# An attention layer's event table: memory loads behind the key copy, output transposes 12 to 15 steps later, last memory mixing and samples' norm moved

## The chip, the core and the metric

The kernel runs on one core of a Trainium2 chip. The metric is the device time of one execution in microseconds (us). Before the change it is 1348.73 us, the median of three runs (1347.39 to 1349.89).

TensorE is called PE here as in the profile; DVE is VectorE, ACT ScalarE, POOL GpSimd, and SP the SyncE queue, which issues the DMAs. Every engine works through its own instructions in program order, and semaphores order the engines against each other.

## The reference

A two-layer encoder trunk for one step: layer 0 mixes tokens with a recurrence (RWKV-7), layer 1 with differential attention. Each layer does one input projection, mixes, attends to a memory of 256 rows with four "memory heads", gates, and does one output projection. 512 prompt rows and 32 sample rows are computed together. The change touches layer 1 alone:

```python
def diff_layer(x, mk, mv, k_past, v_past, layer_idx, ...):
    h = rmsnorm(x, norm_w)
    q, k, v, qm, gate = jnp.split(h @ w_in, [...], axis=-1)
    ...
    # per head: softmax(q1 k1) - lam * softmax(q2 k2), masked, times v
    o = rmsnorm(o, subln) * (1.0 - lam_init)
    y_mem = mem_attention(qm, mk, mv)        # 4 heads, 256 memory rows
    out = jnp.concatenate([o, y_mem], axis=-1) * jax.nn.silu(gate)
    return x + out @ w_out, k, v
```

The prompt rows attend to prompt keys and use memory keys made in this kernel; the 32 sample rows also use cached keys and values (128 rows) and cached memory keys and values (256 rows).

## The kernel before, in words

**Main stream.** Layer 1 is written as one stream of PE matmuls, the input projection: each block of 128 output columns is 48 matmuls (weights 128x128, 272 rows of tokens at a time; `6 * KT = 48`). One such matmul is called a step. Twelve attention heads follow each other; head h owns three blocks (value, key, query), some gate blocks, and in heads 1, 3, 5 and 7 (`MEM1`) the query and gate of a memory head. The function `begin(h)` gives the step at which a head starts: heads 7, 8, 9, 10 and 11 start at steps 1632, 1872, 2064, 2208 and 2352, for example. After step 2688 the output projection follows.

**Events.** Everything else (transposes, scores, softmax, copies, DMAs, norms) is an event: `at(pos, fn)` in `diff_layer` (from L2041) puts a function into the list `ev`, the list is sorted, and each function is called just before step `pos` of the stream. Its instructions then stand at that place in the program of every engine that it uses. There is no other scheduler: tables of numbers at the file's head set the order. "h9+122" below means 122 steps after the start of head 9.

**One head's events on the SP queue.** The prompt's weights stream in all the time as `h16s` tiles. Head h then sends, at fixed steps: at +99 the keys are made, at +108 `keys_out` (L2122) copies the half of the keys across partitions (`kh<-kh`, two DMAs, needed by the scores `ps_s` from +160 on) and stores the keys (`scr<-sg`, four). At +112 `weights_out` (L2191) of the head before stores its attention weights (`ptr<-pk`, four DMAs of 160 KB), and at +168 `weights_back` reads them back transposed (`aT<-ptr`).

**Memory heads.** `mem_steps` (L1233) is a generator whose pieces are called at the offsets of `MEMAT1` (L41; the last memory head has `MEMAT1B`, L42). The second piece issues four loads on SP: `cmt` (cached memory keys), `mhk`, `mhv`, `cmv`. The third, at +180, transposes `cmt` on PE into the PSUM tile `ps_ck`. Scores, softmax and turning follow, and the last piece is the mixing: `ps_mo` on PE, then two DVE operations that write the gated tile `og`.

**Groups of four heads.** Attention outputs are normalized and transposed for four heads at a time, while the heads after them run: `norms` (L2308), then for j = 0 to 3 `scaled` (L2313, DVE `ot`) and `finished` (L2327: four PE transposes into `ps_oT`, then two DVE operations that write the gated tile `og`). For the second group (heads 4 to 7) that falls into heads 9 and 10, for the last one to the end of head 11. `gated_square` (L1428, ACT, at `GSQUARE`) and `gated_scales` (L1434, at `GSCALE`) take a scale from the finished tiles; the latter's PE result is `ps_gs`.

**Samples.** Also once in four heads the samples' attention is computed (`SAMPLE1`, L53, and `SAMPLE2`, L54, for the last group): scores, mixing, `sample_norm` (L2296, ten small DVE operations on `os`) and `sample_rows` (L2302, PE transpose `ps_osT`). In head 9, `cached_keys` (L2244) transposes the cached keys of the next group on DVE (`to<-ck`) at h9+4; the load of `ck` is issued at h8+152.

**PSUM.** `ps_ck`, `ps_mo`, `ps_oT`, `ps_osT` and `ps_gs` come from one pool, `psm`, of two banks: a tile waits until the one but last of them is read out.

All instructions are recorded through a small wrapper, so that rows of the profile show line 138 (139 after the change) whatever function issued them; the names of tiles tell them apart.

Of the kernel before, what the change touches and what calls it, by code (L numbers as in the profile page):

```python
# [37 lines left out]
GATES1[11] = (8, 9, 10, 11)  # L38
MEM1 = (1, 3, 5, 7)
TILES1 = ((160,180),(188,210),(220,244),(254,280))  # L40
MEMAT1 = (60, 64, 180, 276, 294, 306, 324, 330, 346, 362, 402, 414, 426, 476, 552)  # L41
MEMAT1B = MEMAT1[:8] + (352, 366, 400, 412, 428, 470, 590)  # L42
LOADS1, SPLITS1 = (1, 14), (2, 5, 8, 11)
STAT1, SPREAD1, POWER1, SCALE1 = (14, 27), 12, 32, (37, 41)
SPLITS2, SCALE2 = (7, 11, 13, 17), (33, 36)
GSQUARE = ((8, 36), (8, 132), (9, 36), (9, 84), (10, 10), (10, 32), (10, 56), (10, 78))
GSCALE = ((9, 132), (10, 92))
KVOUT = 164
GSPLIT = ((10, 36, 57), (10, 66, 89), (11, 33, 57), (11, 66, 89), (11, 222, 230), (11, 254, 262), (11, 290, 298), (11, 318, 325))
ORDERED = (2 * KT - 2) * 6 * KT + 3 * KT  # L50
EXP = float(1 << 23)
ROOT = float(0x5F3759DF) + 14 * EXP
SAMPLE1 = ((310, "s"), (338, "m"), (362, "t"), (386, "w"), (406, "n"), (464, "r"))  # L53
SAMPLE2 = ((186, "s"), (214, "m"), (228, "t"), (264, "w"), (311, "n"), (336, "r"))  # L54
TILES2 = ((152, 180), (210, 236), (240, 268), (272, 304))
BACK1, SUMS1, NORM1 = 80, 160, 52
# [84 lines left out]
class Trunk:  # L141
# [1899 lines left out]
    def diff_layer(self, dq, p, mp, mctx, pool_early, tiles, consume):  # L2041
# [8 lines left out]
        def at(pos, fn):  # L2050
            ev.append((pos, len(ev), fn))
# [13 lines left out]
        def make_v(st):  # L2065
            def make(w):
                st["v"] = dq.tile([P, T], F32, tag="v", name="v", bufs=KB)
                yield from self.steps(w, copied(st["v"], w[2]))
            return make

        def make_k(st):
            def make(w):
                st["k"] = dq.tile([P, T], F32, tag="k", name="k", bufs=KB)
                yield from self.steps(w, copied(st["k"], w[2]))
            return make

        def make_q(st):
            def make(w):
                st["qp"] = qp = dq.tile([P, 2, T], F32R, tag="qp", name="qp", bufs=QB)

                def parts(ps, c):
                    for m in range(2):
                        self.ae.activation(qp[rows[m], m, c], ps[rows[m], :], AF.Copy, scale=w[2][rows[m]])
                    if c.start:
                        self.ae.activation(st["G"]["qs"][:, st["j"], :], ps[:, TH - TS :], AF.Copy, scale=w[2])
                    for m in range(2):
                        self.ve.scalar_tensor_tensor(qp[rows[1 - m], m, c], ps[rows[m], :], w[2][rows[m]],
                                                       qp[rows[m], m, c].bitcast(F32), ALU.mult, ALU.subtract)
                yield from self.steps(w, parts)
            return make  # L2090

        def make_gate(g):
            def make(w):
                half[g] = w[2]
                self.ve.tensor_scalar(subg[:, g : g + 1], self.subs, w[2], None, ALU.mult)
                yield from self.steps(w, self.gate_evac(self.o1[g], w[2])[2])
            return make
# [125 lines left out]
        def opened(G, hg):  # L2223
            G["scr"] = [self.dp.tile([T, 4, P], F32, tag=f"scr{i}", name=f"scr{i}", bufs=3) for i in range(2)]
            G["on"] = []
# [94 lines left out]
        def turned_stored(G, j):  # L2320
            G["ot", j] = G["ot", j]()
# [5 lines left out]
        def finished(G, hg, j):  # L2327
            if hg < OTURN:
                x = G.pop(("oT", j))[:].rearrange("p t q -> p (t q)")
            else:  # L2330
                ps = self.psm.tile([P, 512], F32, tag="m", name="ps_oT")
                for t in range(4):
                    self.te.transpose(ps[:, t * P : t * P + P], G["on"][j][:, t, :], self.ident[:])
                x = ps[:]
            g = self.o1[4 * hg + j]
            n = 4 * hg + j
            self.ve.scalar_tensor_tensor(g[:, :TP], x, subg[:, n : n + 1], g[:, :TP], ALU.mult, ALU.mult)
            self.ve.scalar_tensor_tensor(g[:, TP:], G["oT"][:, 32 * j : 32 * j + 32], half[n], g[:, TP:], ALU.mult, ALU.mult)
# [10 lines left out]
        for h, st in enumerate(sts):  # L2349
            f, hg, G = len(makes) * 6 * KT, h // 4, groups[h // 4]  # L2350
            start.append(f)
            makes += [make_v(st), make_k(st), make_q(st)] + [make_gate(g) for g in GATES1.get(h, ())]
            if h % 4 == 0:
                at(f, lambda G=G, hg=hg: opened(G, hg))
                at(f + 97, lambda G=G: sample_open(G))
                at(f + 152, lambda G=G, hg=hg: cached(G, hg))
            if h % 4 == 1:
                for off, fn in ((4, cached_keys), (14, cached_stored), (78, cached_back)) if CTURN else ((124, cached_turned),):
                    at(f + off, lambda G=G, fn=fn: fn(G))
            for off, fn in ((52, values_turn), (62, lambda st: st["vout"]()), (99, keys), (108, keys_out)):  # L2360
                at(f + off, lambda st=st, fn=fn: fn(st))
            last = h == DH - 1
            for t, (x, y) in enumerate(TILES2 if last else TILES1):
                at(f + x, lambda st=st, t=t: scores(st, t))
                at(f + x + 6, lambda st=st, t=t: powers(st, t))
                at(f + (y - (14, 0, 0, 10)[t] if last else y), lambda st=st, t=t, fn=joined if last else turned: fn(st, t))
                if last:
                    at(f + y + 12, lambda st=st, t=t: turned_here(st, t))
            back, sums = (BACK2, SUMS2) if h >= DH - 2 else (BACK1, SUMS1)
            for off, fn in ((124, values_back),) if last else ((y + min(18, back - 2), values_back), (y + (8 if h == DH - 2 else OUT7[0] if h == 7 else OUT1), weights_out), (y + (OUT7[1] if h == 7 else back), weights_back)):  # L2370
                at(f + off, lambda st=st, fn=fn: fn(st))
            if h == 7:
                sums = OUT7[2]
            at(f + y + (SUMS3 if last else sums), lambda st=st: weighted(st))
            at(f + y + (SUMS3 + 11 if last else sums + 14), lambda st=st: squared(st))
            if h in MEM1:
                m = MEM1.index(h)
                makes += [make_query(mems[m]), make_mem_gate(mems[m], m)]
                for off in MEMAT1B if h == MEM1[-1] else MEMAT1:
                    at(f + off, lambda m=m: next(mits[m], None))  # L2380
            if h % 4 == 3:
                for off, fn in (SAMPLE2 if last else SAMPLE1):
                    fn = {"s": sample_scores, "m": sample_mixed, "t": sample_turned, "w": sample_weighted, "n": sample_norm, "r": sample_rows}[fn]
                    at(f + off, lambda G=G, fn=fn: fn(G))
                b = f + y + NORM2 if last else begin(h + 2) + (NORM1 if h < 4 else NORM1B)
                at(b, lambda G=G: norms(G))
                for j in range(4):
                    if hg >= OTURN and not last:
                        x = b + 18 + (14, 24)[hg] * j
                        at(x, lambda G=G, j=j: scaled(G, j))  # L2390
                        at(x + (36 + 10 * j, 38)[hg], lambda G=G, hg=hg, j=j: finished(G, hg, j))
                    elif last:
                        at(b + 18 + 8 * j, lambda G=G, j=j: scaled(G, j))
                        at(b + 48 + 14 * j, lambda G=G, hg=hg, j=j: finished(G, hg, j))
                    else:
                        x = b + 18 + STEP * j
                        at(x, lambda G=G, j=j: (scaled(G, j), turned_out(G, j)))
                        at(x + 10, lambda G=G, j=j: turned_stored(G, j))
                        at(x + GAP1, lambda G=G, j=j: turned_back(G, j))
                        at(x + GAP2, lambda G=G, hg=hg, j=j: finished(G, hg, j))  # L2400
            if h == 10:
                we = []
                at(f + 34, lambda: (mctx.close(), we.append(pool_early())))
        for g, (h, off) in enumerate(GSQUARE):
            at(begin(h) + off, lambda g=g: self.gated_square(g))
        for g, (h, x, y) in enumerate(GSPLIT):
            at(begin(h) + x, lambda g=g: self.gated_split(g, we[0], tiles))
            at(begin(h) + y, lambda g=g: self.gated_rest(g, tiles))
        for g, (h, off) in zip((0, 4), GSCALE):
            at(begin(h) + off, lambda g=g: self.gated_scales(g, 4))  # L2410
# [129 lines left out]
```

## Time and profile before

| what | value |
|---|---|
| profiled execution, its own time | 1346.43 us |
| its span (first to last instruction) | 1343.9 us |
| lies around the span | 2.5 us |
| runs | 1347.39, 1348.73, 1349.89 us |
| mean granted TensorE clock | 0.992 |
| PE busy | 96% of the span |
| DVE, ACT, POOL busy | 71%, 66%, 50% |
| mean DMA rate | 128 GB/s |
| HBM read, written | 130.84 MB, 41.92 MB |

How to read it: a timeline row gives the start in us, the duration in us, the engine, the operation, what it writes and reads, and how many like it stand in the row; brackets at the end give the idle time ahead of it and what ended that. An SP row (SPq) is the issue of a DMA, not its transfer. A row of the waits names who waited for whom, the total in us, the number of waits, and the longest. A row of the windows gives, after the stretch and its length, the busy time of PE, PEld, DVE, ACT and POOL (with instructions), then the granted clock, the DMA engines' busy share and GB/s. Layer 1's stream runs from about 824 us to 1233 us, its last group and the output projection from there to 1344 us.

### The profile page before, as it was taken

Reading aid. Unit: us, or ns where it says so; the run is one execution under the profiler, and the core shown is the slowest. Engines: PE = TensorE matmul, PEld = TensorE weight load, DVE = VectorE, ACT = ScalarE, POOL = GpSimd, SP = SyncE. Lnnn points to the kernel's source line nnn. Section 1 sums busy time; section 2 is a strip of 40 time slices with the busy share of each in tenths; the row PEclk is TensorE's granted clock in tenths of the full one; section 3 lists DMA queues with packets and bytes.
Section 4 is the critical chain, followed back from the end, with each engine's and each line's share of the span. In section 5 each row is a group of like instructions: output and inputs, shape, how many; then the busy total and the mean of one; then the engine's idle time right before and its main releaser. Section 6 shows DMA issues by size and latency. Waiting matters only on the chain. (4 is left out here: it accounts for less than half of the span.)

```text
span 1343.9 us, 32356 instructions
## 1 busy us (share of the span) xinstructions
PE 1295.0 (96%) x11776; PEld 1169.3 (87%) x11776; DVE 950.2 (71%) x2483; ACT 888.6 (66%) x2412; POOL 676.6 (50%) x1139
## 2 busy tenths in 40 slices
PE   6999999999999999999999999999999999999996
PEld 6998989999999999888899999888887887788885
DVE  6767667887788777767575355656698667987855
ACT  6665677777777867656564337777666777886752
POOL 1317765577557655860021007756555655654651
PEclk9999899999999999999999999999999999999998
DMA  7643223322322332233347445777777768874741
GB/s 236 187 115 82 63 71 88 79 67 80 88 68 65 81 101 62 60 81 98 124 150 224 132 130 153 173 175 165 155 177 170 169 164 179 174 166 115 225 149 67
DMA packets 418298, 171.55 MB, mean 128 GB/s; under 512 B 195209, under 2 KB 402578, under 8 KB 418138
## 3 DMA queue, kind: packets, MB, share of 16 engines
q1 hardware_dynamic: 417994, 168.96, 48.7%
q8 instruction: 92, 1.51, 0.5%
q14 instruction: 68, 0.56, 0.1%
q10 hardware_dynamic: 144, 0.52, 0.1%
HBM read 130.84 MB, written 41.92 MB: 129 GB/s over the span
## 5 line engine op out<-in xcount | busy, mean ns | idle before, releaser
L138 PEld LDWEIGHTS <-whs 128*128 128x128 f16 x3456 | 327.0, 98 | 67.2 <-issue 5.2
L138 PE MATMUL ps_g<-h,whs 128*128 128x272 f16 x2688 | 332.0, 279 | 1.3 <-POOL whs L138 1.3
L138 PE MATMUL ps_g<-hh,wlo 128*128 128x272 f32 x912 | 277.4, 304 | 1.3 <-DVE wlo L138 1.3
L138 PE MATMUL ps_g<-hh,whi 128*128 128x272 f32 x912 | 274.6, 301 | 0.9 <-ACT hh L138 0.9
L138 PE MATMUL ps_g<-hl,whi 128*128 128x272 f32 x912 | 270.9, 297 | 0.6 <-POOL hl L599 0.5
L888 POOL TENSOR_TENSOR tm<-u,m 102x84 f32<-102x84 f32 (+23 forms) x372 | 156.5, 421 | 164.4 <-DMA m<-sc 136.4
L138 PEld LDWEIGHTS ps_g<-hh,whi 128*128 128x128 f32 x912 | 174.2, 191 | 4.4 <-ACT hh L138 1.3
L138 PEld LDWEIGHTS ps_g<-hh,wlo 128*128 128x128 f32 x912 | 173.6, 190 | 4.8 <-DVE wlo L138 2.1
L138 PEld LDWEIGHTS ps_g<-hl,whi 128*128 128x128 f32 x912 | 173.5, 190 | 2.4 <-POOL hl L599 0.7
L890 POOL TENSOR_TENSOR u<-u,tm 102x84 f32<-102x84 f32 (+23 forms) x372 | 159.7, 429 | 29.1
L138 POOL TENSOR_TENSOR whs<-h16s,whs 128x512 f16<-128x512 f32 x126 | 147.8, 1191 | 51.1 <-ACT whs L138 45.9
L138 DVE TENSOR_TENSOR wlo<-raw,whi 128x512 fp32r<-128x512 f32 x178 | 128.8, 734 | 47.3 <-ACT whi L138 46.3
L138 ACT CAST whi<-raw 128x512 fp32r<-128x512 f32 x178 | 107.0, 616 | 35.3 <-issue 19.4
L138 POOL TENSOR_SCALAR h16s<-h16s 128x512 f32<-128x512 f32 x112 | 81.4, 739 | 91.9 <-DVE h16s L138 91.9
L138 ACT CAST whs<-h16s 128x512 f16<-128x512 f32 x144 | 84.7, 618 | 31.7 <-POOL h16s L138 30.1
L138 PE MATMUL ps_g<-hl,whs 128*128 128x272 f16 x768 | 93.2, 279 | 0.5 <-POOL whs L138 0.5
L138 ACT ACTIVATE junkw<-h16s 128x512 bf16<-128x512 f32 x138 | 86.4, 627 | 5.7 <-DMA h16s<-in_df_in_dram 5.3
L138 DVE SCALAR_TENSOR_TENSOR SB<-ps_c,dl,sd 64x64 f32<-64x64 f32 x168 | 47.4, 282 | 42.2 <-PE ps_c L138 38.2
L138 PE MATMUL ps_g<-lo,whi 128*128 128x272 f32 x256 | 73.9, 289 | 0.7 <-DVE lo L138 0.7
L138 PE MATMUL ps_g<-hi,whi 128*128 128x272 f32 x256 | 73.7, 288 | 0.0
L138 PE MATMUL ps_g<-hi,wlo 128*128 128x272 f32 x256 | 73.5, 287 | 0.0
L138 ACT COPY sv<-ps_c 64x64 f32<-64x64 f32 x192 | 39.3, 205 | 39.1 <-PE ps_c L138 37.3
(413 smaller groups left out, 2934.5 us busy)
## 6 DMA issues: line engine op xcount, KB each, us to landing
raw<-in_rw_in_dram SPq DMA_DIRECT2D x114, 256.0 KB
h16s<-in_df_in_dram SPq DMA_DIRECT2D x112, 256.0 KB
raw<-in_w_out_dram SPq DMA_DIRECT2D x32, 256.0 KB
h16s<-in_w_out_dram SPq DMA_DIRECT2D x32, 256.0 KB
ptr<-pk SPq DMA_DIRECT2D x44, 160.0 KB
aT<-ptr SPq DMA_DIRECT2D x11, 640.0 KB
scr<-sg SPq DMA_DIRECT2D x96, 68.0 KB
out_dram<-scr SPq DMA_DIRECT2D x6, 1024.0 KB
```

The source lines that it names most:

```text
L138: return lambda *a, **k: self.trunk.tie(self, issue(*a, **k))
L888: nc.gpsimd.tensor_tensor(tm[:, :n, :wd], u3[:, :n, kx : kx + 1].to_broadcast(sh), m3[:, kx : kx + 1, kx + 1 :].to_broadcast(sh), ALU.mult)
L890: nc.gpsimd.tensor_tensor(u3[:, :n, kx + 1 :], u3[:, :n, kx + 1 :], tm[:, :n, :wd], ALU.add)
```

## The change

Five edits, all to offsets of events; no operation is added or removed.

1. `MEMAT1[1]`, also used by `MEMAT1B`, goes from 64 to 124: the four memory loads of heads 1, 3, 5 and 7 are issued 60 steps later. The transposes that read `cmt` stay at +180.
2. The last entry of `MEMAT1B` goes from 590 to 554: the last memory head's mixing moves from h10+14 to h9+122.
3. The new table `SAMPLE1B` holds for the second group: `sample_norm` goes from h8+166 to h9+8, `sample_rows` from h9+32 to h9+44.
4. The second group's `finished` goes from h9+132, h10+12, h10+36, h10+60 to h9+146, h10+26, h10+50, h10+74, with its `GSQUARE` and `GSCALE` entries.
5. The last group's `finished` goes 12 steps later (four times).

```diff
-MEMAT1 = (60, 64, 180, 276, 294, 306, 324, 330, 346, 362, 402, 414, 426, 476, 552)
-MEMAT1B = MEMAT1[:8] + (352, 366, 400, 412, 428, 470, 590)
+MEMAT1 = (60, 124, 180, 276, 294, 306, 324, 330, 346, 362, 402, 414, 426, 476, 552)
+MEMAT1B = MEMAT1[:8] + (352, 366, 400, 412, 428, 470, 554)
...
-GSQUARE = ((8, 36), (8, 132), (9, 36), (9, 84), (10, 10), (10, 32), (10, 56), (10, 78))
-GSCALE = ((9, 132), (10, 92))
+GSQUARE = ((8, 36), (8, 132), (9, 36), (9, 84), (10, 24), (10, 46), (10, 70), (10, 93))
+GSCALE = ((9, 132), (10, 106))
...
 SAMPLE1 = ((310, "s"), (338, "m"), (362, "t"), (386, "w"), (406, "n"), (464, "r"))
+SAMPLE1B = SAMPLE1[:4] + ((440, "n"), (476, "r"))
...
-                for off, fn in (SAMPLE2 if last else SAMPLE1):
+                for off, fn in (SAMPLE2 if last else SAMPLE1 if h < 4 else SAMPLE1B):
...
-                        at(x + (36 + 10 * j, 38)[hg], lambda G=G, hg=hg, j=j: finished(G, hg, j))
+                        at(x + (36 + 10 * j, 52)[hg], lambda G=G, hg=hg, j=j: finished(G, hg, j))
...
-                        at(b + 48 + 14 * j, lambda G=G, hg=hg, j=j: finished(G, hg, j))
+                        at(b + 60 + 14 * j, lambda G=G, hg=hg, j=j: finished(G, hg, j))
```

On SP, in head 3 (heads 1, 5 and 7 are alike): `cmt`, `mhk`, `mhv`, `cmv` are the memory loads, `vt` the values read back, `scr` the keys' store. Before:

```order
L138 DMA cmt<-in_cache_mem_k_dram 128x2x128
L138 DMA mhk<-mkv_11874 128x256
L138 DMA mhv<-mkv_12091 128x256
L138 DMA cmv<-in_cache_mem_v_dram 128x2x128
L138 DMA h16s<-in_df_in_dram 128x4x128
L138 DMA vt<-scr_12367 128x4x128
L138 DMA kh<-kh 64x544 x2
L138 DMA scr_12366<-sg_83 32x17x32 x4
L138 DMA h16s<-in_df_in_dram 128x4x128
L138 DMA ptr<-pk 32x40x32 x4
L138 DMA h16s<-in_df_in_dram 128x4x128 x2
```

On SP, in the same place of head 3, now:

```order
L139 DMA h16s<-in_df_in_dram 128x4x128 x2
L139 DMA vt<-scr_12367 128x4x128
L139 DMA kh<-kh 64x544 x2
L139 DMA scr_12366<-sg_83 32x17x32 x4
L139 DMA h16s<-in_df_in_dram 128x4x128
L139 DMA ptr<-pk 32x40x32 x4
L139 DMA cmt<-in_cache_mem_k_dram 128x2x128
L139 DMA mhk<-mkv_11874 128x256
L139 DMA mhv<-mkv_12091 128x256
L139 DMA cmv<-in_cache_mem_v_dram 128x2x128
L139 DMA h16s<-in_df_in_dram 128x4x128 x2
```

The four loads moved from ahead of the key copy `kh<-kh` to a place behind it, behind the four stores `scr` and behind the four large stores `ptr<-pk`.

On DVE, at the end of head 8, the samples' norm before (`os` and `nt` are its tiles, `og` a gate, `ps_s` the scores of head 8):

```order
L138 TENSOR_REDUCE snm<-ps_s 128x1 x2
L138 TENSOR_SCALAR os_16620<-os_16620 128x1 x2
L138 SCALAR_TENSOR_TENSOR nt_16862<-os_16620 128x1
L138 TENSOR_TENSOR nt_16862<-nt_16862,os_16620 128x1
L138 SCALAR_TENSOR_TENSOR os_16620<-nt_16862,os_16620 128x1
L138 TENSOR_TENSOR nt_16862<-os_16620 128x1
L138 TENSOR_TENSOR nt_16862<-nt_16862,os_16620 128x1
L138 SCALAR_TENSOR_TENSOR nt_16862<-nt_16862 128x1
L138 SCALAR_TENSOR_TENSOR os_16620<-nt_16862,os_16620 128x1
L138 TENSOR_SCALAR os<-os,os_16620 128x128
L138 SCALAR_TENSOR_TENSOR og_12336<-og_12336,ps_g 128x272
L138 STREAM_TRANSPOSE to<-mp 128x256
```

On DVE, at the start of head 9, the samples' norm now (`to<-ck` is the transpose of the cached keys):

```order
L139 TENSOR_REDUCE snm<-ps_s 128x1 x2
L139 SCALAR_TENSOR_TENSOR og_12336<-og_12336,ps_g 128x272
L139 STREAM_TRANSPOSE to<-ck 128x512
L139 TENSOR_SCALAR os_16620<-os_16620 128x1 x2
L139 SCALAR_TENSOR_TENSOR nt_16946<-os_16620 128x1
L139 TENSOR_TENSOR nt_16946<-nt_16946,os_16620 128x1
L139 SCALAR_TENSOR_TENSOR os_16620<-nt_16946,os_16620 128x1
L139 TENSOR_TENSOR nt_16946<-os_16620 128x1
L139 TENSOR_TENSOR nt_16946<-nt_16946,os_16620 128x1
L139 SCALAR_TENSOR_TENSOR nt_16946<-nt_16946 128x1
L139 SCALAR_TENSOR_TENSOR os_16620<-nt_16946,os_16620 128x1
L139 TENSOR_SCALAR os<-os,os_16620 128x128
```

The norm moved across the border of heads 8 and 9 and now stands right behind `to<-ck`.

## The prediction

> **What bounds the kernel now.** I read the page first, then the stretch of layer 1's main stream in the windows, with one window inside head 1, and then whom PE waits for from 824 us to the end.
>
> ```profile
> PE 1295.0 (96%) x11776; PEld 1169.3 (87%) x11776; DVE 950.2 (71%) x2483; ACT 888.6 (66%) x2412; POOL 676.6 (50%) x1139
> ```
> ```profile
> 824.00:1233.00 409.00, 403.03 (x3512) 337.06 (x3512) 290.16 (x874) 297.35 (x819) 243.24 (x248) 1.00 0.74 168
> 863.00:872.00 9.00, 8.98 (x78) 7.45 (x77) 4.55 (x19) 8.19 (x23) 7.95 (x9) 1.00 0.99 215
> ```
> ```profile
> PE ps_oT L138 <- DVE ot L138: 2.0, 2, 1.1
> PE ps_g L138 <- POOL whs L138: 1.8, 3, 0.8
> PE ps_s L138 <- DMA kh<-kh: 1.0, 1, 1.0
> ...
> PE ps_mo L138 <- DVE og L138: 0.9, 1, 0.9
> PE ps_s L138 <- ACT pt L138: 0.9, 1, 0.9
> ```
>
> PE is the bound: busy for 403.03 of the stream's 409.00 us. So what happens on another engine counts only where PE is made to wait. The edits aim at five of these waits, some 5 us in all, and that is all they can win. The second window shows what they may disturb: behind the keys of head 1 the DMA engines are 0.99 busy. A load that joins the queue there waits for what is ahead of it.
>
> **Edit 1: the memory loads.** They now stand on SP behind `ptr<-pk`. `aT<-ptr` reads what `ptr` wrote, so SP's issue of `aT` marks when `ptr` has landed. Here are SP and PE in head 1, then in head 3, and SP's wait ahead of `kh<-kh` in head 3:
>
> ```profile
> 868.48 3.69 SPq L138 DMA_DIRECT2D ptr<-pk  x4
> ...
> 875.21 0.37 SPq L138 DMA_DIRECT2D aT<-ptr  x1
> ```
> ```profile
> 871.34 0.38 PE L138 MATMUL ps_ck<-ident,cmt 128*128 128x128 f32 x2
> ```
> ```profile
> 938.18 3.64 SPq L138 DMA_DIRECT2D ptr<-pk  x4
> ...
> 944.86 0.37 SPq L138 DMA_DIRECT2D aT<-ptr  x1
> ```
> ```profile
> 940.98 0.97 PE L138 MATMUL ps_g<-h,whs 128*128 128x272 f16 x7
> 941.79 0.38 PE L138 MATMUL ps_ck<-ident,cmt 128*128 128x128 f32 x2
> ```
> ```profile
> SPq L138 <- ACT kh L138: 2.2, 1, 2.2
> ```
>
> In head 3 the issue of `ptr` ends at 938.18 + 3.64 = 941.82, so `cmt`, now next, is issued just when PE wants it (941.79). Does a load queued behind `ptr` land ahead of it? Head 8 has such a case, a weight load right behind `ptr`, with ACT waiting for it:
>
> ```profile
> 1122.38 0.98 SPq L138 DMA_DIRECT2D h16s<-in_df_in_dram  x1
> ...
> 1127.39 0.44 SPq L138 DMA_DIRECT2D aT<-ptr  x1
> ```
> ```profile
> 1127.63 0.63 ACT L138 ACTIVATE junkw<-h16s 128x512 bf16<-128x512 f32 x1 [1.30 <-DMA h16s<-in_df_in_dram]
> ```
>
> It was issued at 1122.38 and used at 1127.63, that is 5.25 us later and 0.24 after `aT`'s issue. So it came in the queue's order, and I put `cmt` at `aT`'s issue + 0.3. PE works in order, so the whole stream stops at `ps_ck`. Heads 5 and 7, the span of the four issues in head 5 among them:
>
> ```profile
> 1004.20 0.52 SPq L138 DMA_DIRECT2D cmt<-in_cache_mem_k_dram  x1
> ...
> 1006.24 0.46 SPq L138 DMA_DIRECT2D ckT<-spread  x1
> ...
> 1021.53 0.37 SPq L138 DMA_DIRECT2D aT<-ptr  x1
> ```
> ```profile
> 1017.84 0.38 PE L138 MATMUL ps_ck<-ident,cmt 128*128 128x128 f32 x2
> ```
> ```profile
> 1090.57 0.37 SPq L138 DMA_DIRECT2D aT<-ptr  x1
> ```
> ```profile
> 1087.97 0.38 PE L138 MATMUL ps_ck<-ident,cmt 128*128 128x128 f32 x2
> ```
>
> The four issues take 1006.24 - 1004.20 = 2.0 us of SP, by which what follows them can be early now. In heads 3 and 7 it can't: SP waits 2.2 us for ACT's `kh` there (the row above; head 7 has the same), and an earlier SP only waits longer. In heads 1 and 5 I take the 2.0 off; taking nothing off is the upper end. Head 5's `ps_ck` comes 1.0 earlier, since its wait for `kh<-kh` (1.0) goes.
>
> - Head 1: 875.21 - 2.0 + 0.3 - 871.34 = 2.2 (up to 4.2).
> - Head 3: 944.86 + 0.3 - 941.79 = 3.4.
> - Head 5: 1021.53 - 2.0 + 0.3 - (1017.84 - 1.0) = 3.0 (up to 5.0).
> - Head 7: 1090.57 + 0.3 - 1087.97 = 2.9.
>
> Sum +11.5 (to 15.5), and -1.0 for `kh<-kh`. The lower end is in the rivals. The other three loads and the `aT` behind them are used at +276 and +248, at least 68 steps behind `ps_ck`; at 0.116 us a step (seven from 940.98 to 941.79) that is 7.9 us, so they stay hidden, and would cost about the 2.0 of their issue if that cover were gone.
>
> **Edits 2 to 4: heads 9 and 10.** The samples' norm, and what it meets:
>
> ```profile
> 1132.63 0.27 PE L138 MATMUL ps_osT<-ident,os 128*128 128x128 f32 x1
> ```
> ```profile
> 1129.17 0.38 SPq L138 DMA_DIRECT2D ck<-in_cache_k_dram  x1
> ```
> ```profile
> 1134.48 0.71 DVE L138 STREAM_TRANSPOSE to<-ck 128x512 f32<-128x512 f32 x1 [3.10 <-DMA ck<-in_cache_k_dram]
> ```
> ```profile
> 1229.08 0.33 DVE L138 TENSOR_SCALAR os<-os 128x1 f32<-128x1 f32 x2
> ...
> 1230.80 0.35 DVE L138 TENSOR_SCALAR os<-os,os 128x128 f32<-128x128 f32 x1
> ```
> ```profile
> PE ps_g L138 <- POOL whs L138: 0.5, 1, 0.5
> ```
>
> Without the norm ahead of it, the scores' wait for `pt` (0.9) goes. But DVE stood idle 3.10 us at `to<-ck`, waiting for a load, and now the norm is queued behind that, with `ps_osT` on PE waiting for it. The norm takes 1230.80 + 0.35 - 1229.08 = 2.07 (last group, nothing between). It can begin when `to<-ck` is done, 1134.48 + 0.71 = 1135.19, and end at 1137.26. PE comes to `ps_osT` 12 steps later than before, less the 0.9: 1132.63 + 12 x 0.116 - 0.9 = 1133.1. So PE stops for +4.1 (0 if `ck` lands 4 us earlier against PE; no row goes above). While it stands, the weights get ahead: the stretch's wait for `whs` (0.5) goes. The mixing's 0.9 and one `ps_oT` of 0.9 (half of the 2.0 of two) go too, since their tiles are asked for later or stand elsewhere. New is that `ps_gs` asks for a bank right behind the mixing:
>
> ```profile
> 1149.54 0.17 PE L138 MATMUL ps_gs<-outt,h16s 128*128 128x4 bf16 x1
> ```
> ```profile
> 1150.76 1.01 DVE L138 SCALAR_TENSOR_TENSOR qp<-ps_g,h16s,qp 64x272 fp32r<-64x272 f32 x2
> ```
>
> The mixing's `og`, which frees the bank, now stands on DVE behind that `qp`, which ends at 1151.77, 2.2 us after `ps_gs` in the trace. Between 0 (DVE gets ahead during the stop) and 2.2 I take the middle, 1.1. Sum: 4.1 + 1.1 - 0.9 - 0.9 - 0.9 - 0.5 = +2.0; from -3.2 to +3.1.
>
> **Edit 5: the last group.** PE waits twice there:
>
> ```profile
> 1239.77 0.66 PE L138 MATMUL ps_oT<-ident,ot 128*128 128x128 f32 x4 [1.05 <-DVE ot L138]
> ...
> 1244.53 0.66 PE L138 MATMUL ps_oT<-ident,ot 128*128 128x128 f32 x4 [0.38 <-DVE og L138]
> ```
>
> Twelve steps are 1.4 us: more than 1.05, so that goes. The 0.38 is DVE's pace in freeing banks, and moves rather than goes; I leave 0.5 of the 1.43 for it: -0.9, from -1.4 to 0.
>
> **The clock.** A stop can cost more than itself. Three windows of the first layer:
>
> ```profile
> 534.70:538.10 3.40, 3.34 (x53) 3.00 (x52) 2.49 (x7) 2.41 (x9) 0.74 (x2) 1.00 0.56 171
> 538.10:541.50 3.40, 3.40 (x17) 3.40 (x17) 3.09 (x11) 2.22 (x8) 2.85 (x8) 0.50 0.25 75
> 541.50:544.90 3.40, 3.39 (x28) 3.16 (x28) 2.22 (x6) 2.11 (x6) 2.77 (x9) 1.00 0.00 0
> ```
>
> The granted clock is 0.50 for 3.40 us, with 17 matmuls in place of 28, so about half of the window is lost: 1.7 us. Ahead of it stand 53 matmuls, most of them tiny: a window used for little. No stop of PE in layer 1 now is over 1.1 us, so its clock of 1.00 shows nothing of stops of 2 to 4 us. I take one such window, for the longest stop: +1.7 (0 to five of them). [...]
>
> **Sum.** 11.5 - 1.0 + 2.0 - 0.9 + 1.7 = +13.3 on the profiled 1346.4, so 1359.7. The runs' median is 2.3 above that execution: 1362.0.
>
> **The rivals,** in times against the median:
>
> - *No half clock.* The same stops, nothing for the clock: 1360.3. For it: the stops are about as short as a window or shorter, so that some work lies in nearly every window. Against it: the row at 534.70, busy and followed by the half clock. 0.25. [...]
> - *Three half clocks.* +3.4: 1365.4. For it: five stops, of 2.2 to 4.1 us. Against it: a stop that falls across the border of two windows leaves work in both, and three of five would have to fall well. 0.17.
> - *The norm's stop doesn't bite.* `ck` lands early enough against PE, whose stops let the queue get ahead; heads 9 and 10 come to -3.2 and no clock is lost: 11.5 - 1.0 - 3.2 - 0.9 = +6.4, 1355.1. For it: `ck` was under way for 1134.48 - 1129.17 = 5.3 us, as long as a load behind `ptr`, so much of it is queueing. Against it: the last stop of edit 1 is some 40 us earlier (1087.97). 0.10.
> - *Faster.* The queue keeps up: with the four loads gone from its front, `ptr` goes out without queueing and `cmt` lands within about 0.5 us of its issue, as soon as issued. Then the stop of head 3 is about 0.5, others none, `ck` is earlier, the norm's stop about 1.0: 0.5 - 1.0 - 3.2 + 1.0 - 0.9 = -3.6, 1345.1. For it: 2.0 us of SP gained in two heads. Against it: the bytes are the same, the engines 0.99 busy, the 5.25 us of head 8. It decides where `cmt` lands less than about 0.5 us after PE's wish. 0.05.
> - *It does nothing.* The stops come to what the waits gave back (about 5 us): 1348 to 1350. 0.04.
>
> **How the numbers follow.** My forecast, one half clock, has 0.39: 1362.0. The range leaves out the last two rivals and the top of the three half clocks, and takes in the upper ends of heads 1 and 5: 1354 to 1368. About 0.2% (2.7 us) is what a measurement of this kernel can tell from no change. The faster rival and a bit of the one that does nothing give 0.06 for faster, the rest of it and of the early-`ck` case 0.06 for the same, and 0.88 is left for slower.
>
> **What would show it.** Right: in the waits of the changed kernel, `ps_ck` waits for DMA `cmt` four times, 2 to 4 us each; `ps_osT` waits for DVE `os` about 4 us; the waits for `kh<-kh`, for ACT `pt` and of `ps_mo` for `og` are gone; one or a few windows at 0.50 behind such a stop. Wrong: `ps_ck` rows of under 1 us, `cmt` landing well ahead of `aT`'s issue, or stops as long as forecast with the span hardly longer, which would mean that PE isn't the bound there.

## The result, and the profile after

The changed kernel takes 1370.47 us (median of 5 runs, 1368.95 to 1373.56), the kernel before 1348.73 (5 runs, 1347.39 to 1351.69). The ratio is 1.0167, with a 95% interval of 1.0152 to 1.0181: slower by 22 us, where the prediction had 13. Ratios, here and below, leave out three executions of later kernels that lie far from all others (1587, 4346 and 7185 us). The profiled execution took 1368.95 us, 22.5 more than the one of before; its span is 1367.2 us, 23.3 more.

The engine row of the changed kernel's page, and then whom PE waits for from 824 us to the end:

```profile
PE 1304.2 (95%) x11776; PEld 1174.7 (86%) x11776; DVE 950.9 (70%) x2483; ACT 888.1 (65%) x2412; POOL 676.2 (49%) x1139
```
```profile
PE ps_ck L139 <- DMA cmt<-in_cache_mem_k_dram: 9.1, 3, 3.4
PE ps_osT L139 <- DVE os L139: 4.2, 1, 4.2
PE ps_ck L139 <- DVE h16s L139: 2.9, 1, 2.9
PE ps_gs L139 <- ACT junkw L139: 2.5, 1, 2.5
PE ps_g L139 <- POOL whs L139: 1.2, 2, 0.8
PE ps_f L139 <- DVE x L139: 1.0, 3, 0.6
PE ps_gs L139 <- DVE og L139: 0.7, 1, 0.7
```

Two things are to be read from them. The five waits that the change aimed at are gone, `kh<-kh`, `pt`, `ps_mo` and both waits of `ps_oT` for `ot`, and six large stops stand in their place. And PE is *busy* for 9.2 us more than before (1304.2 against 1295.0) with the same 11776 matmuls, while DVE, ACT and POOL are busy as before. A stop is idle time and isn't counted as busy, so the stops alone don't explain this. What does is PE's clock, shown below.

SP and PE in head 3 of the changed kernel:

```profile
942.85 3.85 SPq L139 DMA_DIRECT2D ptr<-pk  x4
946.75 0.95 SPq L139 DMA_DIRECT2D cmt<-in_cache_mem_k_dram  x1
...
951.36 0.46 SPq L139 DMA_DIRECT2D aT<-ptr  x1
```
```profile
950.23 0.44 PE L139 MATMUL ps_ck<-ident,cmt 128*128 128x128 f32 x2 [3.06 <-DMA cmt<-in_cache_mem_k_dram]
```

`cmt` is issued when the four `ptr` are out, at 946.75, and PE goes on at 950.23, 3.5 us later. In the other heads it is 3.1 to 4.0 us; head 1's stop is 3.37, head 7's 2.71. In the third row of the waits, head 5's, the profile names DVE. I count it with the others, since `cmt` had been issued 3.7 us before PE went on, as in the other heads, and since all four stops are named as `cmt`'s when edit 1 stands alone (below):

```profile
1025.87 0.87 SPq L139 DMA_DIRECT2D cmt<-in_cache_mem_k_dram  x1
```
```profile
1029.54 0.66 PE L139 MATMUL ps_ck<-ident,cmt 128*128 128x128 f32 x2 [2.88 <-DVE h16s L139]
```

The clock shows in windows. The first three are cut where the granted clock changes around the stop of head 1:

```profile
872.46:875.87 3.41, 0.68 (x6) 0.61 (x7) 1.18 (x5) 0.20 (x1) 1.36 (x2) 1.00 0.82 196
875.87:879.28 3.41, 3.41 (x17) 2.58 (x16) 0.82 (x4) 0.53 (x2) 0.00 (x0) 0.50 1.04 285
879.28:882.70 3.42, 3.42 (x32) 2.94 (x30) 1.80 (x5) 3.37 (x11) 1.80 (x2) 1.00 0.85 218
```

A window of 3.41 us with PE busy for 0.68 is followed by one at 0.50, which is busy throughout and does 17 matmuls. In the trace's records of the clock, such a window stands behind each of the six large stops: at 875.9, 951.0, 1029.5, 1104.6, 1155.8 and 1275.2. Before, there is none between 541.5 and 1336.8, shortly ahead of the end. Six times 1.7 are 10.2 us, about what PE is busier. The mean granted clock was 0.985 in this execution and 0.982 to 0.985 in the four others, so the profiled one is not an unlucky one.

### The profile page after: what moved, and what is told of

The parts are those of the page before. It is cut to its first block, busy times and chain, and to the rows that moved or that the text cites. A ratio compares the mean times of both kernels' runs of the same rounds, so it can differ in the third digit from the quotient of the medians.

```text
span 1367.2 us, 32366 instructions
## 1 busy us (share of the span) xinstructions
PE 1304.2 (95%) x11776; PEld 1174.7 (86%) x11776; DVE 950.9 (70%) x2483; ACT 888.1 (65%) x2412; POOL 676.2 (49%) x1139
## 5 line engine op out<-in xcount | busy, mean ns | idle before, releaser
L139 PE MATMUL ps_g<-h,whs 128*128 128x272 f16 x2688 | 337.8, 282 | 0.8 <-POOL whs L139 0.8
```

Of the source, the lines that this page charges most:

```text
L139: return lambda *a, **k: self.trunk.tie(self, issue(*a, **k))
```

## The experiments

Times are medians against runs of the kernel before on the same chip (1348.8 to 1349.7); the ratios have a 95% interval. Fourteen kernels were measured.

### Each half of the change by itself

Edit 1 alone:

```diff
-MEMAT1 = (60, 64, 180, ...)
+MEMAT1 = (60, 124, 180, ...)
```

> The kernel before with edit 1 alone. The local theory: the change's cost sits in six stops of PE, each with its own cause (four at ps_ck behind the late cmt, one at ps_osT behind the norm, one at the last ps_gs), and each stop of over 2.5 us is followed by one half-clock window of 1.7 us. It expects here four ps_ck stops of together 12.1 us, four half clocks (6.8) and the 1.0 of kh<-kh gone: +17.9 us, 1366.6. The rival that the half clocks come of something else expects +11.1, 1359.8. The rival that the stops of heads 9 to 11 also come of the disturbed queue expects stops there too: 1369 or more.

Measured 1369.25 us, 1.0145 (1.0127 to 1.0162): +19.6. PE's waits in its profile:

```profile
PE ps_ck L138 <- DMA cmt<-in_cache_mem_k_dram: 14.6, 4, 4.0
```

Four stops, each with a window at 0.50 behind it (the mean granted clock is 0.986, against 0.992 before), and the other waits of layer 1 much as in the kernel before, without the one for `kh<-kh`. So edit 1 makes these stops alone. They are 2.5 us longer than in the changed kernel (12.0 there). That isn't the load's own time: from the issue of `cmt` to its use it is 3.0 to 3.8 us in the four heads, as in the changed kernel (3.1 to 4.0). SP issues it 0.3 to 0.9 us later against PE in each head; why is not settled.

Edits 2 to 5 without it (the changed kernel with 64 in place of 124):

> The changed kernel with the loads back at +64, so edits 2 to 5. The local theory expects no ps_ck stop, and the stops at ps_osT (4.2 us) and at the last ps_gs (2.5) with a half clock each: 1370.5 - 17.9 = 1352.6. If those stops came of the disturbed queue they are gone with the loads back in place, and the edits 2 to 5 win their 3 to 4 us: 1345 to 1346.

Measured 1356.52, 1.0052 (1.0036 to 1.0069): +6.9, against 3.9 expected.

```profile
PE ps_osT L139 <- DVE os L139: 3.9, 1, 3.9
PE ps_gs L139 <- ACT junkw L139: 2.5, 1, 2.5
PE ps_gs L139 <- DVE og L139: 1.5, 1, 1.5
```

The stops of heads 9 to 11 stand here too, so they aren't a consequence of the disturbed queue. The two halves add up to 26.5, 4.8 more than the whole (21.7 by the medians). The longer stops just named make 2.5 of it, and a small stop that one half shows (1.5 at `ps_gs`) is shorter in the whole (0.7). But the whole has one half-clock window more than the halves together (six against four and one), so some 3 us of the difference stay open. The 3.9 at `ps_osT` had no half clock behind it here, which led to the question below, which stops cost the clock.

### Where the loads may stand

The loads behind the key copy, but ahead of `ptr`:

```diff
-MEMAT1 = (60, 64, 180, ...)
+MEMAT1 = (60, 110, 180, ...)
```

> The kernel before with the memory loads at +110: behind the key copy and its stores, but ahead of ptr<-pk. The local theory (cmt waits for the 640 KB of ptr ahead of it in the queue) expects ps_ck stops of at most 1.0 us each, no half clock, and the wait for kh<-kh gone: 1347.5 to 1351. The rival, that any load issued in that jammed stretch comes too late whether ahead of ptr or behind, expects four stops of 2 us or more: 1358 or more.

Measured 1352.52, 1.0021 (1.0007 to 1.0034), above the 1347.5 to 1351 expected. No stop at `ps_ck`, as the theory said, but new ones:

```profile
PE ps_o L138 <- DMA aT<-ptr: 5.4, 3, 2.3
```

The four loads push `ptr` back on SP, so `aT`, which reads it, comes late: against PE's `ps_ck`, the issue of `ptr` ends 1.8 to 2.2 us later than before in heads 1, 3 and 7, whose `ps_o` wait, and 0.4 later in head 5, whose `ps_o` doesn't. At +64, in heads 3 and 7, they pass in time in which SP waits 2.2 us for `kh` anyway; behind that wait they are in the way of whatever is next. The 2.3 us stop, in head 1, was followed by a half-clock window too, though none was expected.

The run shows that a load ahead of `ptr` is in time. It doesn't show by itself that `cmt` queues behind the bytes of `ptr`: in head 1 it was issued 4.6 us ahead of its use here, and the 3.0 to 4.0 us seen behind `ptr` would have been enough. Most of what makes it late in the changed kernel is that SP needs 3.8 to 4.5 us for the issues of `ptr` ahead of it.

The changed kernel, with the reader later:

```diff
-MEMAT1 = (60, 124, 180, ...)
+MEMAT1 = (60, 124, 230, ...)
```

> The changed kernel with the transposes that read cmt at +230 in place of +180 (50 steps, 5.8 us), the loads still at +124. The local theory expects no ps_ck stop, since cmt lands 3.4 us late at most: the same as with the loads back, about 1352.6. The rival, that the loads behind ptr also delay what is queued behind them (aT and the weights), expects waits of PE for aT or whs and half clocks with them: 1358 or more.

Measured 1357.93, 1.0063 (1.0040 to 1.0087), 5 above what the local theory expected. The 12 us at `ps_ck` and their clock are gone, some 12.5 of the change's 22. But the rival is right in part:

```profile
PE ps_o L139 <- DMA aT<-ptr: 5.1, 3, 2.4
PE ps_osT L139 <- DVE os L139: 4.4, 1, 4.4
PE ps_gs L139 <- ACT junkw L139: 2.5, 1, 2.5
```

In the changed kernel the stop at `ps_ck` covered a late `aT`; without that stop, `aT` ends last. The prediction had `aT` hidden by 7.9 us. That cover was there only because PE stood still.

### When a stop halved the clock

Edit 1, with the reader 12 steps later:

```diff
-MEMAT1 = (60, 64, 180, ...)
+MEMAT1 = (60, 124, 192, ...)
```

> The kernel before with the loads at +124 as in edit 1, and the transposes that read cmt at +192 (12 steps, 1.4 us later than in edit 1 alone, which had stops of 4.0, 3.4, 3.9 and 3.2 us and four half clocks). Theory A, from the runs so far: the clock is halved for a window of 3.41 us when PE stood still for 2.1 us or more of the window ahead (2.14 and more did it, 1.97 and less didn't). The stops shrink to 2.6, 2.0, 2.5 and 1.8, of which at most two can fill a window so far: +9.0 - 1.0 and 0 to 3.4 for the clock, 1357 to 1360. Theory B, that each stop is followed by a half clock whatever its length: four windows, 1363.5.

Measured 1354.35, 1.0045 (1.0032 to 1.0058): 15 us less than with the reader at +180, for 12 steps (1.4 us) at four places, and below what either theory expected. No half clock from 824 us on up to the end of the output projection, and

```profile
PE ps_ck L138 <- DMA cmt<-in_cache_mem_k_dram: 6.1, 4, 2.6
```

8.5 of the 15 are the stops (14.6 to 6.1), and 6.8 would be four half-clock windows. So theory B falls. The stops were expected to shrink by 5.6 us, not by 8.5: `cmt` again took 3.1 to 3.8 us from issue to use, but in heads 3, 5 and 7 SP was ahead by more than the 12 steps give, which isn't explained. Three of the four stops are now under 2 us (1.64, 0.48 and 1.42).

What did the windows ahead of a half clock look like? In the changed kernel the half-clock windows lie on one grid of 3.41 us, wherever the stops begin: the six starts, given above, are 75.1, 78.5, 75.1, 51.2 and 119.4 us apart, that is 22, 23, 22, 15 and 35 times 3.41. In the window ahead of each, PE is busy for 0.60 to 0.88 us; in every other full-clock window from 824 us on and up to the last 12 us it is busy for 2.02 us or more. Cut on such a grid, here are the two windows that the stop of 2.59 in head 1 of this kernel spans and the one behind, then the same for the 3.9 at `ps_osT` in edits 2 to 5:

```profile
872.57:875.98 3.41, 1.84 (x16) 1.37 (x14) 2.95 (x13) 0.89 (x3) 1.36 (x2) 1.00 0.73 123
875.98:879.39 3.41, 2.39 (x22) 2.07 (x23) 0.52 (x3) 1.91 (x7) 0.03 (x1) 1.00 0.87 255
879.39:882.80 3.41, 3.41 (x30) 2.85 (x29) 2.18 (x9) 2.86 (x9) 2.25 (x2) 1.00 1.12 296
```
```profile
1136.73:1140.14 3.41, 1.44 (x13) 0.98 (x10) 0.78 (x3) 1.10 (x3) 1.11 (x1) 1.00 1.12 286
1140.14:1143.55 3.41, 1.50 (x13) 1.29 (x14) 3.02 (x16) 0.72 (x2) 0.00 (x0) 1.00 0.84 156
1143.55:1146.97 3.42, 3.42 (x32) 3.28 (x31) 2.91 (x10) 2.85 (x9) 1.36 (x2) 1.00 0.91 234
```

and for a stop of 2.54 at the last `ps_gs`, in the kernel with edit 5 alone (below):

```profile
1255.81:1259.22 3.41, 1.36 (x14) 1.02 (x12) 0.24 (x1) 3.41 (x12) 0.33 (x2) 1.00 0.46 169
1259.22:1262.63 3.41, 2.92 (x14) 1.94 (x14) 2.33 (x8) 2.18 (x7) 0.60 (x1) 0.50 0.29 93
```

A stop of 3.9 us that falls evenly on two windows, busy for 1.44 and 1.50, cost no clock, nor did the one of 2.59, with 1.84 and 2.39; one of 2.54 that leaves 1.36 in one window (2.05 idle) did. So the length of a stop doesn't tell by itself. The stop at the last `ps_gs` shows it too: it is 2.5 us long in six of the kernels and cost a half clock in five of them, but not in the kernel with the scale ahead of the mixing (below), where its two windows were busy for 2.32 and 1.98. A stop of 4.37 (the reader at +230) cost two windows. The half-clocked one behind it was again part idle, with 2.10 busy, more than the 1.44 that kept the full clock in edits 2 to 5, so these figures don't tell what ends a half clock:

```profile
1139.43:1142.84 3.41, 0.35 (x4) 0.06 (x1) 1.28 (x6) 1.73 (x5) 0.78 (x1) 1.00 1.06 239
1142.84:1146.25 3.41, 2.10 (x10) 1.40 (x11) 3.12 (x14) 0.11 (x2) 0.00 (x0) 0.50 0.84 162
1146.25:1149.67 3.42, 3.42 (x17) 3.18 (x16) 2.91 (x9) 3.42 (x10) 1.71 (x3) 0.50 1.02 269
```

All this was measured with large matmuls around the stops, 128x272 for the most part, and it is a handful of windows. The first layer's half clocks, behind windows that the records show as busy with many small matmuls (53 in 3.34 us, before), don't fit it, and neither do the last windows of the kernels: one that was busy for 1.76, part of it with six matmuls of 128x1, was followed by the half clock (edit 5 alone). The first layer's half clocks also come and go between executions (from 180 us on, four in the profile of edit 4 alone, one in that of before).

### The samples' norm

Edits 2 to 5, with the norm ahead of `to<-ck`:

```diff
-SAMPLE1B = SAMPLE1[:4] + ((440, "n"), (476, "r"))
+SAMPLE1B = SAMPLE1[:4] + ((435, "n"), (476, "r"))
```

> Edits 2 to 5 with the loads at +64 (the kernel that came to 1356.5 us, with a stop of 3.9 us at ps_osT), and the samples' norm at h9+3, one step ahead of to<-ck, in place of h9+8. The local theory (the norm is queued behind to<-ck, which waits for a load) expects the stop at ps_osT gone: 1352 to 1353. The rival, that ps_osT is late for another reason (DVE's load at the head's start, a bank), expects a stop of 2 us or more: 1355 or more.

Measured 1354.30, 1.0034 (1.0017 to 1.0050), 2.2 less than with the norm behind and above the 1352 to 1353 expected. The stop at `ps_osT` is down to 0.4, so its cause was the place behind `to<-ck`. In the changed kernel DVE shows the chain plainly:

```profile
1152.42 0.71 DVE L139 STREAM_TRANSPOSE to<-ck 128x512 f32<-128x512 f32 x1 [4.53 <-DMA ck<-in_cache_k_dram]
1153.05 0.30 DVE L139 TENSOR_SCALAR os<-os 128x1 f32<-128x1 f32 x2
...
1154.74 0.35 DVE L139 TENSOR_SCALAR os<-os,os 128x128 f32<-128x128 f32 x1
```

DVE stands 4.53 us for a load, with a norm behind it that doesn't need the load, and PE behind the norm (until 1155.15). But not all of the 3.9 was won, since the next wait grew from 1.5 to 2.4, now with a half clock:

```profile
PE ps_gs L139 <- ACT junkw L139: 2.5, 1, 2.5
PE ps_gs L139 <- DVE og L139: 2.4, 1, 2.4
```

### The memory mixing and the second group's transposes

That kernel, with `gated_scales` of head 9 ahead of the mixing, so that `ps_gs` doesn't ask for the bank that the mixing holds:

```diff
-GSCALE = ((9, 132), (10, 106))
+GSCALE = ((9, 118), (10, 106))
```

> The kernel with the norm ahead of to<-ck and the loads at +64 (1354.3 us), whose ps_gs in head 9 stood 2.4 us for the mixing's og on DVE, with a half clock, and now gated_scales at h9+118 in place of h9+132, ahead of the mixing at h9+122. The local theory (ps_gs asks for the bank that the mixing's og frees) expects that stop and its half clock gone: 1354.3 - 4.1 = 1350.2. The rival, that DVE's lateness there stops PE at the next tile of psm anyway, expects a wait of 1.5 us or more at ps_oT or ps_s of heads 9 and 10: 1353 or more.

Measured 1352.77, 1.0029 (1.0015 to 1.0043). The rival holds: the wait only went to the next tile of the pool, from DVE's `og` at `ps_gs` to DVE's `outs` at `ps_mo`, and kept its half clock:

```profile
PE ps_gs L139 <- ACT junkw L139: 2.5, 1, 2.5
PE ps_mo L139 <- DVE outs L139: 2.2, 1, 2.2
```

Then each of the two edits alone. Edit 2:

```diff
-MEMAT1B = MEMAT1[:8] + (..., 470, 590)
+MEMAT1B = MEMAT1[:8] + (..., 470, 554)
```

> The kernel before with edit 2 alone: the last memory mixing at h9+122, where DVE works through the second group's norm and its ot tiles. The theory that the mixing's og is late there (PE then waits about 2 us for a bank of psm, whatever tile asks for it) expects the 0.94 of ps_mo gone, a stop of 1.5 to 2.5 us at ps_gs or ps_oT and a half clock where a window has 2.05 us of it: +0.6 to +3.3, 1349.5 to 1352.5. The rival, that the stop comes only of the transposes standing later (edit 4), expects the 0.94 won: 1348.

Measured 1350.03, 1.0017 (1.0003 to 1.0031), with a stop of 2.4 us and a half clock behind it:

```profile
PE ps_oT L138 <- DVE og L138: 2.8, 2, 2.4
```

Edit 4, the second group's `finished` 14 steps later with its `GSQUARE` and `GSCALE` (these lines of the diff alone):

> The kernel before with edit 4 alone: the second group's finished 14 steps later, its squares and second scale too. The theory that blames the mixing expects the 0.9 of ps_oT won, the mixing at h10+14 as before, no new stop over 1 us: 1348. The rival that blames edit 4 expects a stop of 1.5 us or more in heads 9 and 10: 1350 or more.

Measured 1347.84, 0.9994 (0.9980 to 1.0009): the wait of `ps_oT` for `ot` in head 9 is gone, but no gain can be told from nothing. One 1.6 us wait for `whs` near 1158 us is new. So it is the mixing at h9+122 that PE pays for. Its two `og` operations stand on DVE behind the second group's norm and `ot`; in the three kernels with this wait (the norm ahead, the scale ahead, edit 2 alone) PE stood in turn at `ps_gs`, `ps_mo` and `ps_oT`, whichever asked for a bank next.

### The last group

Edit 5 alone:

```diff
-                        at(b + 48 + 14 * j, lambda G=G, hg=hg, j=j: finished(G, hg, j))
+                        at(b + 60 + 14 * j, lambda G=G, hg=hg, j=j: finished(G, hg, j))
```

> The kernel before with edit 5 alone (last group's finished 12 steps later). The local theory: the wait of 1.05 at ps_oT goes, the eight squares that are due at steps 24 to 108 of the output projection start only when the last finished has been issued (step 104 in place of 92), so the last ps_gs at step 142 waits 2.5 us for them, with a half clock: -1.0 + 2.5 + 1.7 = +3.2, 1352 to 1353. The prediction on record has -0.9 for this edit: 1348.

Measured 1353.67, 1.0030 (1.0017 to 1.0042).

```profile
PE ps_gs L138 <- ACT junkw L138: 2.5, 1, 2.5
```

How it comes about: the output projection has its own list of events, the eight squares of gates 8 to 15 among them, due at its steps 24 to 108, and the scale `ps_gs` at step 142. But its loop starts only when the attention's list is empty, that is behind the last `finished`: 12 steps later now, at step 104. All squares due by then go to ACT in one burst: seven in a row before, eight in the changed kernel. ACT and PE before, then in the changed kernel:

```profile
1246.10 0.64 ACT L138 ACTIVATE junkw<-og 128x544 bf16<-128x544 f32 x1
```
```profile
1253.03 0.17 PE L138 MATMUL ps_gs<-outt,h16s 128*128 128x8 bf16 x1
```
```profile
1269.03 0.62 ACT L139 CAST whs<-h16s 128x512 f16<-128x512 f32 x1 [2.90 <-POOL h16s L139]
1269.56 0.65 ACT L139 ACTIVATE junkw<-og 128x544 bf16<-128x544 f32 x1
...
1274.04 0.64 ACT L139 ACTIVATE junkw<-og 128x544 bf16<-128x544 f32 x1
```
```profile
1274.83 0.17 PE L139 MATMUL ps_gs<-outt,h16s 128*128 128x8 bf16 x1 [2.53 <-ACT junkw L139]
```

Before, the burst began 6.9 us ahead of `ps_gs` and was done in time. Now a weight's cast that waits 2.90 us for POOL has got in ahead of it, and the eight squares end at 1274.68. The squares of the four memory gates don't depend on the last group, and as events of the attention's list they go out at their due steps:

```diff
+        for i in range(4):
+            at(begin(12) + 24 + 12 * i, lambda g=12 + i: self.gated_square(g))
...
-                after(24 + 12 * i, self.gated_square, g)
+                if g < 12:
+                    after(24 + 12 * i, self.gated_square, g)
```

> Edit 5 alone, and the squares of the four memory gates (12 to 15) issued at their due steps 24 to 60 as events, so that only four of the eight squares stand behind the last finished. The local theory (the burst of eight on ACT makes ps_gs late) expects the stop at the last ps_gs gone and the 1.05 won: 1348 to 1349. The rival, that the last og itself comes too late for step 142, expects a stop of 1 us or more at ps_gs: 1350 or more.

Measured 1350.43, 1.0000 (0.9981 to 1.0019). No wait at `ps_gs` is left in its profile, so the burst was the cause. The time is above the 1348 to 1349 expected: the 1.05 won at `ps_oT` can't be told from nothing.

### Is there a faster version?

The norm ahead, the scale ahead of the mixing, and the squares at their due steps together, with the loads at +64:

> The same, and the squares of the four memory gates at their due steps, as in the run that freed the last ps_gs. The local theory expects the stop of 2.5 us at the last ps_gs and its half clock gone as well: 1350.2 - 4.2 = 1346, that is 3 us or 0.2% below the kernel before, by the waits that edits 2 to 5 were aimed at. If costs come back elsewhere, it is no faster than before.

Measured 1349.92, 1.0008 (0.9996 to 1.0021), not the 1346 expected: the last `ps_gs` no longer waits, `ps_mo` still does (2.2 us and a half clock). The same with the loads behind `aT` and the reader at +236:

> The same with the memory loads at +170, two steps behind weights_back (aT<-ptr) in place of +64, and the transposes that read cmt at +236. The theory that loads placed ahead of aT delay it (5 us of waits of PE for aT where the loads stood at +110 or +124 and the reader didn't wait) expects no wait for aT, none at ps_ck (the load has 66 steps, 7.7 us), and the wait for kh<-kh (1.0) gone: 1345. If a load there also queues for 5 us and mhk is late for the scores at +276, waits at ps_mm appear: 1348 or more.

Measured 1353.03, 1.0037 (1.0023 to 1.0050), not the 1345 expected: no wait for `aT` nor for `kh<-kh`, but `ps_ck` still waits:

```profile
PE ps_ck L139 <- DMA cmt<-in_cache_mem_k_dram: 2.4, 3, 1.2
```

Where it waits, `cmt` took 5.5 to 5.7 us from issue to use, behind `aT` now (640 KB). These waits don't make up the 3 us against the kernel without that edit; the rest stays open, since its one profile was taken at a granted clock of 0.943 on average and its waits of PE aren't compared with the others. Last, edits 4 and 5 with the squares at their due steps, and nothing else:

> Edits 4 and 5 with the squares of the memory gates at their due steps; the mixing, the norm and the loads as before. If the two waits at ps_oT are won and nothing comes back: 1348.9 - 1.9 = 1347. If gains of under 1 us are taken back at the next wait: 1349.

Measured 1348.10, 0.9995 (0.9979 to 1.0012). No version here is faster than the kernel before by more than the measurement can tell.

## Why the prediction was wrong

The direction was right, and so were five of the six large stops with their causes. The price of the clock and the last group were wrong: the time is 8.5 us short (1362.0 against 1370.5), and beyond the range. Step by step, in the changed kernel's profile:

- **The stops at `ps_ck`: right.** 2.2, 3.4, 3.0 and 2.9 forecast, 11.5 in all; 3.37, 3.06, 2.88 and 2.71 measured, 12.0. Head 1's 1.2 has two parts: SP was 1.5 us earlier against PE there, not 2.0, and `cmt` took 4.0 us from its issue, where the forecast comes to 3.3. The mark used for the landing did not carry over: PE used `cmt` 0.2 to 1.1 us ahead of the issue of `aT`, which SP now reaches too late to wait for `ptr`. What held is the 3.3 us behind the last `ptr` that the mark gave before. The -1.0 for `kh<-kh` came too.
- **Heads 9 and 10: right.** 4.1 forecast at `ps_osT`, 4.2 measured; 1.1 at `ps_gs`, 0.7 measured. The five waits gone are as listed. The cause of the first was shown by moving the norm, that of the second by the mixing alone and the scale ahead of it.
- **The clock: the step that failed.** "I take one such window, for the longest stop: +1.7" became six windows, 10.2 us: 8.5 short. That it equals the whole miss is chance, since the other terms were off as well and the medians don't lie alike against the profiled executions. The price of a window was right. The count was wrong, since the prediction asked whether a stop fills a window, and took one. The windows ahead of the six half clocks weren't idle throughout: they had 0.60 to 0.88 us of 3.41 busy, and one with 1.36 was followed by the half clock in edit 5 alone. Taking the 2.05 us of idle time of that one as enough, a stop of 2.5 leaves that in about half of its positions on the grid, one of 3.4 in four of five, one of 4.2 in all (an estimate from these 2.05 and 3.41 us, for a stop with PE busy around it). By it that makes about four for the six stops as measured, so that all six were followed by the half clock is in part chance; and between three and four for the five stops as forecast. Before had no such window to read this from between 824 us and its last 12 us (the least busy one had 2.36 us), but reasons for more than one did stand in the prediction: five stops of 2.2 to 4.1 us, and a row with the half clock behind a window that was not idle. The rival with three half clocks was still too low.
- **The last group: the other step that failed.** "-0.9" became +1.5 (1.05 won, 2.53 lost), and one of the six half clocks. The prediction followed the moved transposes to who waits for them on PE and DVE, and not to the loop that waits for the list to be empty. The profile of before shows it: seven of the eight squares stand there in one row, though they are due 12 steps apart.
- **A cover that was none.** "They stay hidden" for `aT` held only as long as PE stood at `ps_ck`. In the changed kernel it cost nothing; where the reader moved it cost 5.1 us.

The terms as measured: 12.0 - 1.0 + 1.6 (heads 9 and 10: 4.2 + 0.7 - 0.9 - 0.9 - 0.9 - 0.6) + 1.5 + 10.2 = 24.3, against a span longer by 23.3; the last microsecond is not assigned.

The rival that the whole change would be faster had the queue wrong: a small load right behind the four `ptr` took 3.1 to 4.0 us from issue to use in all four heads. Whether it waits there for the bytes of `ptr`, or would take as long without them, no run tells; behind `aT` it took 5.5 to 5.7.

## What to carry to other kernels

In this kernel, where PE sets the time, the six large stops had a second price, the clock behind them, 1.7 us a window. So what a shorter stop won was more than the stop shows: with the reader 12 steps later the four stops went from 14.6 to 6.1 us, and the time by 15 us. In another kernel the clock behind the stops is to be read from its own profile. Moving a load past a queue's large transfers wants the look at both sides: who reads this load, and who reads what now stands behind it. And before a late event is moved later still, look for what starts only when the list is empty.

## What the runs showed of the hardware

- From 824 us on and up to the last 12 us of the changed kernel, the six windows of 3.41 us with PE busy for 0.60 to 0.88 were each followed by one at 0.50, and no full-clock window with 2.02 or more was. In edit 5 alone, a window with 1.36 was followed by one at 0.50. These are windows of large matmuls; behind windows with small ones among them, busy for 1.76 (edit 5 alone) and even 3.34 (before, at 534.70), the half clock came too. A stop of 2.5 us at the last `ps_gs` cost a half clock in five kernels and none in a sixth, and 3.9 us at `ps_osT`, split 1.44 and 1.50, cost none.
- The issue of four `ptr` took SP 3.85 us, and a load of 128 KB behind them 3.5 us more until PE used it (head 3). In three kernels, twelve such loads took 3.0 to 4.0 us, while the stops they caused lay between 0.5 and 4.0 by how far ahead they were issued. With the loads at +64 the same load caused no wait: the waits of the kernel before have no row for `ps_ck`.
